# Two reorderings in a two-layer hybrid encoder: the third projection tile's weights are split ahead of the first row's scaling and convolution, and the closing norm takes the last row's squares as a second matmul operand

## The chip, the core and the metric

The kernel runs on one core of one Trainium2 chip. The number that counts is the device time of one execution in microseconds (us); the time of a kernel is the median of several executions. Of one execution there is also a profile: when each instruction ran on which engine, what it waited for, and the clock that the throttle granted to the matmul engine. The engines are PE (matmul; its weight loads are listed apart as PEld), DVE (vector), ACT (scalar, activation functions), POOL (GpSimd) and SP (which here only issues DMAs). Each engine works through its own instructions in a fixed order; an instruction that waits holds up all behind it on that engine.

## The reference

Sixteen learned tokens are put before the 1024 tokens of the input (1040 columns of 1024 channels), then two layers run, then a last norm:

```python
h = jnp.concatenate([meta, x], axis=1)
for l in range(DEPTH):
    h = h + hybrid_mixer(rmsnorm(h, norm1_w[l]), w_in[l], conv_qkv_w[l], ...)
    h = h + swiglu(rmsnorm(h, norm2_w[l]), w_gate_up[l], w_down[l])
h = rmsnorm(h, final_norm_w)
return h[:, N_META:]

def rmsnorm(x, w):
    return x * lax.rsqrt(jnp.mean(x * x, axis=-1, keepdims=True) + RMS_EPS) * w
```

In `hybrid_mixer` one projection gives q, k and v of four heads, among others; each of their channels goes through a convolution over three neighbouring tokens and a SiLU, and q and k are then scaled to length one per head:

```python
qkv = jax.nn.silu(depthwise_conv_centred(qkv, conv_qkv_w))
q, k, v = jnp.split(qkv, 3, axis=-1)
k = l2norm(k.reshape(Bsz, L, DN_HEADS, DN_HEAD_DIM))
```

All of it is float32.

## The kernel before

Channels lie on the 128 partitions and tokens in the free dimension, so a row of the kernel's text is a tile of 128 channels by 1040 tokens. A float32 matmul is made from three fast ones: each operand is split into a rounded part (`hi`) and the rest (`lo`), and `dense` (L144 to L171) sums hi*hi, hi*lo and lo*hi for eight blocks of 128 input channels. A projection tile is thus 24 matmuls for each of three column chunks (348, 346 and 346 wide).

The weights of a tile come in two halves of four blocks each. `wsplit` (L122) loads one half from memory (L127, on SP's queue), rounds it on ACT (L128, `whi<-raw`) and subtracts on DVE (L129, `wlo<-raw,whi`). There are three buffers each for `whi` and `wlo` and two for `raw`.

**The start of layer 0.** The scale of the first norm (`rstd`, one number for each token) needs the squares of all of x, and is there only after a chain of sums on PE (L259), a square root on ACT (L215), a reciprocal on DVE (L216) and two DMAs (L217, L219). Meanwhile the loop over `seq` (L644 on) projects tiles 4, 5, 6, 7 (the four k heads) and then 0 to 3 (q). For tiles 4 and 5 the sums are copied out unscaled (L307), and the whole row is scaled later (L653); from tile 6 on the scale is applied on the way out of PSUM (L302). After that the row goes through `conv`: ACT multiplies by the middle tap (L314), DVE adds the two neighbours (L315, L316). For k rows follow SiLU (L639) and the squares (L640) on ACT, and later, as a queued job, a short PE sum of these squares (`sums`, L613). With the fourth k head's sum, `normalise` takes the root (L415) and the reciprocal (L416), POOL's queue writes the lengths out and reads them back spread over the partitions (L418, L421), and DVE scales each k head (L422). `k_out` transposes k on PE (L430, for all four heads of 16 or 128 tokens each) and ACT copies the result out (L432); `chunk_p` multiplies k with itself (L458). After tile 6 the gates are computed (`gates`, L343 on, with its matmuls at L349).

**The end.** The last four blocks of the down projection and the final norm run by column chunk (`FIN`: 512, 256 and 256 columns wide) over eight rows m. For each row: 12 matmuls (L155 to L157), an add to the residual on DVE (L924), the squares on ACT (L186, L180 for the first row), their running sum in `ss` on DVE (L187), and a multiplication by the norm's weight on ACT (L1446). After eight rows `final_scale` sums `ss` over the partitions (PE, L196), takes root (L198) and reciprocal (L199), builds a diagonal (L201) and spreads it over the partitions by another matmul (L204, bank `bc`). DVE then multiplies the eight rows by it (L1450) and SP stores them in pairs (L1451).

**What sets the order.** The program is traced in this order, with priorities, and a scheduler (`schedule_with_timeline_sim=True`) then orders the instructions of each engine by its own forecast of when they can run. A small change in the text can so move instructions some hundred rows away. `after(ins, prev)` adds a dependency by hand: `ins` may not run before `prev`.

Of the kernel before, what the change touches and what calls it, by code (L numbers as in the profile page):

```python
# [7 lines left out]
F32 = mybir.dt.float32  # L8
# [3 lines left out]
ALU = mybir.AluOpType  # L12
# [30 lines left out]
def trunk(ctx: ExitStack, tc: tile.TileContext, xT, w_in, w_ba, w_out, w_gu, w_dn,  # L43
# [75 lines left out]
    evp = [None]  # L119
    jobs, jobs2, jobs3 = [], [], []  # L120

    def wsplit(src, hi, lo, raw=None):  # L122

        kk = src.shape[1]
        if raw is None:
            raw = wp.tile([128, WK, 128], F32, tag="raw", bufs=2, name=nm("raw"))
        dma(raw[:, 0:kk, :], src)  # L127
        act(out=hi, in_=raw[:, 0:kk, :], func=AF.Copy)  # L128
        tt(out=lo, in0=raw[:, 0:kk, :], in1=hi.bitcast(F32), op=ALU.subtract)  # L129

    def wload(src, nk):

# [55 lines left out]

    cols = {}

    def final_scale(ss, n0, n1):

        nt = (n1 - n0) // 128
        ps = bank("a")
        for j in range(nt):
            mm(ps[:, j:j + 1], ss[:, n0 + 128 * j:n0 + 128 * j + 128], ones[:, 0:1], start=True, stop=True)  # L196
        r = sb.tile([128, 4], F32, tag="st", bufs=2, name=nm("rt"))[:, 0:nt]
        act(out=r, in_=ps[:, 0:nt], func=AF.Sqrt, scale=1.0 / D, bias=cols["eps"])  # L198
        nc.vector.reciprocal(out=r, in_=r)  # L199
        dg = t2k("dg")[:, 0:nt, :]  # L200
        tt(out=dg, in0=ident.unsqueeze(1).to_broadcast([128, nt, 128]), in1=r.unsqueeze(2).to_broadcast([128, nt, 128]), op=ALU.mult)  # L201
        bc = bank("b")
        for j in range(nt):
            mm(bc[:, 128 * j:128 * j + 128], ones, dg[:, j, :], start=True, stop=True)  # L204
        return bc[:, 0:n1 - n0]

    def finish_bc(ss, n0, n1, dst, ps=None):

# [77 lines left out]
    for l in range(DEPTH):  # L286
# [23 lines left out]
        def trow():  # L310
            return row(Y[1], F32, 3)

        def conv(src, dst, wc):
            act(out=dst, in_=src, func=AF.Copy, scale=pcol(wc + 1))  # L314
            stt(out=dst[:, 1:L], in0=src[:, 0:L - 1], scalar=pcol(wc), in1=dst[:, 1:L], op0=ALU.mult, op1=ALU.add)  # L315
            stt(out=dst[:, 0:L - 1], in0=src[:, 1:L], scalar=pcol(wc + 2), in1=dst[:, 0:L - 1], op0=ALU.mult, op1=ALU.add)  # L316

# [320 lines left out]
        def lengths(which, q, row_, buf):  # L638
            act(out=row_, in_=row_, func=AF.Silu)  # L639
            act(out=buf, in_=row_, func=AF.Square)  # L640
            jobs.append(lambda: sums(which, q, buf))

        seq = (4, 5, 6, 7, 0, 1, 2, 3)
        for pos, i in enumerate(seq):  # L644
            hh = pos % 4
            if pos == 2:
                gate_weights()
                evp[0] = base - 60000
            t = trow()
            late = pos < (2, 1)[l]  # L650
            inproj(i, to_row_late(t) if late else to_row(t), pfirst if l == 0 and pos == 1 else None)
            if late:
                tt(out=t, in0=t, in1=rstd, op=ALU.mult)  # L653
# [258 lines left out]
        for i in range(4):  # L912
# [6 lines left out]
                tt(out=yl[:, n0:n1], in0=t[:, n0:n1], in1=yh[:, i, n0:n1].bitcast(F32), op=ALU.subtract)  # L919
            ys.append((yh[:, i, :], yl))  # L920

        def add_h(m, then=None):
            def f(ps, n0, n1):
                tt(out=hr[m][:, n0:n1], in0=ps, in1=hr[m][:, n0:n1], op=ALU.add)  # L924
                if then is not None:
                    then(n0, n1)
            return f
# [508 lines left out]
        if not last:  # L1436
            for m in range(KT):
                then = next_norm(m, x[m], par[:, (l + 1) * P_L + P_N1 + m:(l + 1) * P_L + P_N1 + m + 1], ss)
                dense(pre.pop(("dn", m)) if m < 2 else wload(w_dn[l, m, :, 2 * NP:FT, :], NF), rest, chunks, add_h(m, then), pwide)
                dma(hd[m], hr[m])  # L1440
        else:
            for (n0, n1) in FIN:
                for m in range(KT):
                    dense(wds[m], rest, [(n0, n1)], add_h(m), pwide)
                    add_sq(hr[m][:, n0:n1], ss[:, n0:n1], m == 0)
                    act(out=hr[m][:, n0:n1], in_=hr[m][:, n0:n1], func=AF.Copy, scale=par[:, 2 * P_L + m:2 * P_L + m + 1])  # L1446
                bc = final_scale(ss, n0, n1)
                for m in range(0, KT, 2):
                    for q in (m, m + 1):
                        tt(out=hr[q][:, n0:n1], in0=bc, in1=hr[q][:, n0:n1], op=ALU.mult)  # L1450
                    dma(out[m:m + 2, :, n0 - 16:n1 - 16].rearrange("m p t -> p m t"), hb[m // 4][:, m % 4:m % 4 + 2, n0:n1])  # L1451
        if not last:
            finish_bc(ss, 0, L, rsd[1])
        hsrc = hd
# [73 lines left out]
```

## Time and profile before

| | |
|---|---|
| median of 3 runs | 2509.69 us (2503.12 to 2511.69) |
| the profiled execution, its own time | 2505.71 us |
| its span in the trace | 2503.9 us |
| PE busy | 2468.2 us, 99% of the span |
| DVE, ACT, POOL busy | 1763.6, 1045.2, 145.7 us |
| granted clock, mean | 0.997 |

The span is what lies between the first and the last instruction of the trace; the execution's own time is 1.8 us longer. A row of the timeline gives the start, the duration, the engine, the line of the kernel, the operation, the output and the inputs by the program's names, and in brackets the idle time of the engine just before the row and what ended it. A float32 matmul that isn't split counts as two passes (`x8` stands for four of them). PE's rows overlap: the time from one start to the next is what one costs.

### The profile page before, as it was taken

The numbers are of one execution on the slowest core, as the hardware profiler recorded it, in microseconds if no ns is written. First come the engines' busy times: TensorE is split into PE (matmuls) and PEld (weight loads), VectorE is DVE, ScalarE is ACT, GpSimd is POOL, SyncE is SP. The second block draws the span as 40 slices with busy tenths as digits, with TensorE's granted clock in tenths as the row PEclk, the third lists the DMA queues.
The fourth block names the chain that finished last, engine by engine and source line by source line (L and its number), as shares of the span: only waits on it lengthen the run. The fifth ranks groups of instructions, "written<-read, shape, count | busy, mean of one in ns | idle before, by whom it ended". The sixth has DMA issues, their size and how long they took to land.

```text
span 2503.9 us, 44660 instructions
## 1 busy us (share of the span) xinstructions
PE 2468.2 (99%) x17468; PEld 2267.7 (91%) x17468; DVE 1763.6 (70%) x3224; ACT 1045.2 (42%) x1933; POOL 145.7 (6%) x222
## 2 busy tenths in 40 slices
PE   8999999999999999999999999999999999999998
PEld 6989999999999999999999988998978888888887
DVE  5688255769877777787666883457798777668775
ACT  5675222435333333444445752224453333334444
POOL 0040101001000000000000301010110000000000
PEclk9999999999999999999999999999999999999999
DMA  3453155623432222673323531456434322238541
GB/s 131 135 169 101 60 185 166 228 77 122 148 111 99 84 82 77 229 231 120 100 96 125 170 107 68 153 173 218 127 126 156 104 84 84 84 107 288 158 138 68
DMA packets 190887, 331.05 MB, mean 132 GB/s; under 512 B 22956, under 2 KB 77028, under 8 KB 190676
## 3 DMA queue, kind: packets, MB, share of 16 engines
q1 hardware_dynamic: 164676, 290.10, 35.3%
q10 hardware_dynamic: 20752, 25.28, 3.1%
q0 software_dynamic: 5248, 12.82, 1.5%
q8 instruction: 137, 2.24, 0.4%
q14 instruction: 74, 0.61, 0.1%
HBM read 250.31 MB, written 77.80 MB: 131 GB/s over the span
## 4 chain that ended last, share of the span: by engine, by line
PE 86%; DVE 3%; DMA 3%; ACT 2%; issue 1%; POOL 1%; SPq 0%; ACTq 0%; DVEq 0%; POOLq 0%
PE pacc L155 9%; PE pacc L157 9%; PE pacc L156 9%; PE pacc L1034 4%; PE pacc L1036 4%; PE pacc L1035 4%; PE pf L1036 3%; PE pf L1034 3%; PE pf L1035 3%; PE pb L1036 3%; PE pb L1034 3%; PE pb L1035 3%; PE pacc L1427 2%; PE pacc L1425 2%; PE pacc L1426 2%; PE pa L1034 1%
## 5 line engine op out<-in xcount | busy, mean ns | idle before, releaser
L155 PE MATMUL pacc<-a,whi 128*128 128x346 f32 (+1 forms) x808 | 263.5, 329 | 8.3 <-ACT whi L128 7.7
L157 PE MATMUL pacc<-a,wlo 128*128 128x346 f32 (+1 forms) x808 | 262.8, 327 | 0.6 <-DVE wlo L129 0.6
L155 PE MATMUL pacc<-b,whi 128*128 128x346 f32 (+2 forms) x672 | 234.1, 349 | 0.9 <-ACT b L918 0.9
L157 PE MATMUL pacc<-b,wlo 128*128 128x346 f32 (+2 forms) x672 | 231.7, 346 | 0.0
L128 ACT ACTIVATE whi<-raw 128x512 fp32r<-128x512 f32 x168 | 105.4, 629 | 291.9 <-PE pacc L156 243.6
L156 PE MATMUL pacc<-a,whi 128*128 128x346 f32 (+1 forms) x688 | 224.1, 326 | 0.0
L156 PE MATMUL pacc<-b,whi 128*128 128x346 f32 (+2 forms) x580 | 200.4, 346 | 0.4 <-DVE b L919 0.4
L155 PEld LDWEIGHTS pacc<-a,whi 128*128 128x128 f32 x808 | 152.4, 189 | 12.6 <-ACT whi L128 8.2
L129 DVE TENSOR_TENSOR wlo<-raw,whi 128x512 fp32r<-128x512 f32 x168 | 117.4, 699 | 64.3 <-ACT whi L128 63.6
L157 PEld LDWEIGHTS pacc<-a,wlo 128*128 128x128 f32 x808 | 152.5, 189 | 2.8 <-issue 1.3
L155 PEld LDWEIGHTS pacc<-b,whi 128*128 128x128 f32 x672 | 126.5, 188 | 10.7 <-issue 1.5
L157 PEld LDWEIGHTS pacc<-b,wlo 128*128 128x128 f32 x672 | 126.4, 188 | 9.3 <-issue 1.3
L156 PEld LDWEIGHTS pacc<-a,whi 128*128 128x128 f32 x688 | 130.0, 189 | 2.8 <-issue 2.4
L1016 ACT ACTIVATE whi<-rw 128x512 fp32r<-128x512 f32 x100 | 62.7, 631 | 154.3 <-DVE rw L1294 47.3
L156 PEld LDWEIGHTS pacc<-b,whi 128*128 128x128 f32 x580 | 109.2, 188 | 8.0 <-issue 0.8
L1016 ACT ACTIVATE b<-rw 128x512 fp32r<-128x512 f32 x64 | 40.2, 631 | 123.1 <-PE pacc L1035 41.8
L1016 ACT ACTIVATE a<-rw 128x512 fp32r<-128x512 f32 x64 | 40.0, 628 | 106.2 <-PE pacc L1035 70.3
L1017 DVE TENSOR_TENSOR wlo<-rw,whi 128x512 fp32r<-128x512 f32 x100 | 68.1, 684 | 4.9 <-ACT whi L1016 4.2
L302 DVE TENSOR_TENSOR a<-pacc,rstd 128x346 f32<-128x346 f32 (+2 forms) x59 | 32.7, 553 | 46.5 <-PE pacc L157 46.5
L302 DVE TENSOR_TENSOR b<-pacc,rstd 128x346 f32<-128x346 f32 (+1 forms) x63 | 32.2, 512 | 45.2 <-PE pacc L157 45.2
L821 DVE TENSOR_TENSOR rec<-rec 128x512 f32<-128x512 f32 x32 | 22.7, 710 | 46.6 <-DMA rec<-dtd 27.8
L1034 PE MATMUL pacc<-b,whi 128*128 128x260 f32 (+1 forms) x172 | 53.0, 308 | 1.9 <-ACT whi L1016 1.2
(981 smaller groups left out, 7923.1 us busy)
## 6 DMA issues: line engine op xcount, KB each, us to landing
raw<-in_w_in SPq DMA_DIRECT2D x112, 256.0 KB, 2.8
rw<-in_w_gu SPq DMA_DIRECT2D x96, 256.0 KB, 2.8
raw<-in_w_gu SPq DMA_DIRECT2D x96, 256.0 KB, 2.8
rec<-vkd SPq DMA_DIRECT2D x61, 256.0 KB, 3.0
rw<-in_w_dn SPq DMA_DIRECT2D x70, 192.0 KB, 3.6
raw<-in_w_out SPq DMA_DIRECT2D x48, 256.0 KB, 2.7
b<-ad SPq DMA_DIRECT2D x45, 260.0 KB, 4.2
a<-ad SPq DMA_DIRECT2D x45, 256.0 KB, 4.4
```

The lines of the kernel that those rows point to most:

```text
L128: act(out=hi, in_=raw[:, 0:kk, :], func=AF.Copy)
L129: tt(out=lo, in0=raw[:, 0:kk, :], in1=hi.bitcast(F32), op=ALU.subtract)
L155: mm(ps[:, :n], wh, xh[:, n0:n1], start=(k == 0), stop=False)
L156: mm(ps[:, :n], wh, xl[:, n0:n1], start=False, stop=False)
L157: mm(ps[:, :n], wl, xh[:, n0:n1], start=False, stop=(k == K - 1))
L302: tt(out=t[:, n0:n1], in0=ps, in1=rstd[:, n0:n1], op=ALU.mult)
L1016: act(out=hi, in_=src, func=AF.Copy)
L1017: tt(out=lo, in0=src, in1=hi.bitcast(F32), op=ALU.subtract)
L1034: mm(ps[:, :CW], w[0][:, k, :], th[:, cs], start=first and k == 0, stop=False, skip_group_check=True)
L1035: mm(ps[:, :CW], w[0][:, k, :], tl[:, cs], start=False, stop=False, skip_group_check=True)
L1036: mm(ps[:, :CW], w[1][:, k, :], th[:, cs], start=False, stop=stop and k == nk - 1, skip_group_check=True)
L1425: mm(ps[:, :CW], wh[:, k, :], th[:, cs], start=st, stop=False, skip_group_check=True)
```

## The change

First, `wsplit` keeps its two instructions in `lastw`. In layer 0 the work on the first row (tile 4) after its projection is held back as `held`; after the projection of the second row (tile 5) the weights of the third tile (6) are loaded and split, and only then `held` runs: the scaling of the first row is ordered behind the last `lo` of those weights, its convolution's ACT instruction behind the last `hi`.

Second, in the end stage the last row's squares are no longer added to `ss`. They stay in a tile `sq`, and `final_scale` takes `ss` and `sq` as two operands that PE sums in the same bank. The scaling of the second column chunk, which stood behind that chunk's `final_scale` in the text, is now written behind the last add of the third chunk.

```diff
+    lastw = [None, None]
     def wsplit(src, hi, lo, raw=None):
...
-        act(out=hi, in_=raw[:, 0:kk, :], func=AF.Copy)
-        tt(out=lo, in0=raw[:, 0:kk, :], in1=hi.bitcast(F32), op=ALU.subtract)
+        lastw[0] = act(out=hi, in_=raw[:, 0:kk, :], func=AF.Copy)
+        lastw[1] = tt(out=lo, in0=raw[:, 0:kk, :], in1=hi.bitcast(F32), op=ALU.subtract)
...
-    def final_scale(ss, n0, n1):
-        nt = (n1 - n0) // 128
+    def final_scale(parts):
+        nt = parts[0].shape[1] // 128
         ps = bank("a")
         for j in range(nt):
-            mm(ps[:, j:j + 1], ss[:, n0 + 128 * j:n0 + 128 * j + 128], ones[:, 0:1], start=True, stop=True)
+            for i, t in enumerate(parts):
+                mm(ps[:, j:j + 1], t[:, 128 * j:128 * j + 128], ones[:, 0:1], start=(i == 0), stop=(i == len(parts) - 1))
...
-        def conv(src, dst, wc):
-            act(out=dst, in_=src, func=AF.Copy, scale=pcol(wc + 1))
+        def conv(src, dst, wc, prev=None):
+            after(act(out=dst, in_=src, func=AF.Copy, scale=pcol(wc + 1)), prev)
...
-            if late:
-                tt(out=t, in0=t, in1=rstd, op=ALU.mult)
-            dst = (QT if i < 4 else KTt)[:, hh, :]
-            conv(t, dst, P_CV + 3 * i)
-            if i >= 4:
-                lengths("k", hh, dst, t)
+            def convolved(hi=None, lo=None, i=i, hh=hh, t=t, late=late):
+                if late:
+                    after(tt(out=t, in0=t, in1=rstd, op=ALU.mult), lo)
+                dst = (QT if i < 4 else KTt)[:, hh, :]
+                conv(t, dst, P_CV + 3 * i, hi)
+                if i >= 4:
+                    lengths("k", hh, dst, t)
+            if l == 0 and pos == 0:
+                held = convolved
+                continue
+            if l == 0 and pos == 1:
+                pre[seq[2]] = wload(w_in[l, seq[2]], KT)
+                held(*lastw)
+            convolved()
...
-                tt(out=hr[m][:, n0:n1], in0=ps, in1=hr[m][:, n0:n1], op=ALU.add)
+                added[0] = tt(out=hr[m][:, n0:n1], in0=ps, in1=hr[m][:, n0:n1], op=ALU.add)
...
-            for (n0, n1) in FIN:
+            bc = None
+            def scaled(n0, n1, prev):
+                for m in range(0, KT, 2):
+                    for q in (m, m + 1):
+                        after(tt(out=hr[q][:, n0:n1], in0=bc, in1=hr[q][:, n0:n1], op=ALU.mult), prev)
+                    dma(out[m:m + 2, :, n0 - 16:n1 - 16].rearrange("m p t -> p m t"), hb[m // 4][:, m % 4:m % 4 + 2, n0:n1])
+            for c, (n0, n1) in enumerate(FIN):
                 for m in range(KT):
                     dense(wds[m], rest, [(n0, n1)], add_h(m), pwide)
-                    add_sq(hr[m][:, n0:n1], ss[:, n0:n1], m == 0)
+                    prev = added[0]
+                    if m < KT - 1:
+                        add_sq(hr[m][:, n0:n1], ss[:, n0:n1], m == 0)
+                    else:
+                        sq = c4k("sq")[:, 0:n1 - n0]
+                        act(out=sq, in_=hr[m][:, n0:n1], func=AF.Square)
                     act(out=hr[m][:, n0:n1], in_=hr[m][:, n0:n1], func=AF.Copy, scale=...)
-                bc = final_scale(ss, n0, n1)
-                for m in range(0, KT, 2):
...
+                    if c == 2 and m == KT - 1:
+                        scaled(*FIN[1], prev)
+                bc = final_scale([ss[:, n0:n1], sq])
+                if c != 1:
+                    scaled(n0, n1, None)
```

Three places in the engines' order, before and after the scheduler has placed the changed text. Its line numbers are shifted by the added lines: L128 is now L130, L314 L317, L415 L418, L464 L467, L639 L642, L640 L643; at the end L924 is L939, L199 L202, L201 L204, L204 L207, L196 L199, L1450 L1462.

ACT at the start of layer 0. `whi_405` and `whi_411` (before), `whi_388` and `whi_394` (now) are the two halves of tile 6's weights, `whi_620` and `whi_626` those of tile 7's; `b_44` is the first row, `b_59` the second, `b_70` (now `b_69`) the third. Before:

```order
L128 ACTIVATE whi_405<-raw_407 128x512
L215 ACT_TABLE_LOAD
L215 ACTIVATE r_304<-pb_228,epsc 128x260
L314 ACTIVATE b_38_169<-b_44_175,par 128x1040
L128 ACTIVATE whi_411<-raw_413 128x512
L639 ACT_TABLE_LOAD
L639 ACTIVATE b_38_169<-b_38_169 128x1040
L640 ACTIVATE b_44_175<-b_38_169 128x1040
```

Now:

```order
L218 ACTIVATE r_304<-pb_228,epsc 128x260
L130 ACTIVATE whi_394<-raw_396 128x512
L130 ACTIVATE whi_620<-raw_622 128x512
L317 ACTIVATE b_38_169<-b_44_175,par 128x1040
L317 ACTIVATE b_38_169<-b_59_309,par 128x1040
L642 ACT_TABLE_LOAD
L642 ACTIVATE b_38_169<-b_38_169 128x1040
L643 ACTIVATE b_44_175<-b_38_169 128x1040
L130 ACTIVATE whi_626<-raw_628 128x512
```

The second half of tile 6's weights, which stood behind the first row's convolution, now stands ahead of it, and the second row's convolution follows at once. On PE the third chunk of tile 5 (24 matmuls, rows 214 to 237, behind tile 6 and part of the gates) now stands ahead of tile 6.

ACT where the k lengths are taken. `pf` holds the sums of squares of k, `b3f` their roots; `ptm` are tiles of the gates' decay, which get exponentials (L464). Before:

```order
L461 DMA ptm_886<-gd_157 16x4x16
L128 ACTIVATE whi_843<-raw_845 128x512
L461 DMA ptm_886<-gd_157 16x4x16
L415 ACT_TABLE_LOAD
L415 ACTIVATE b3f_763<-pf_342,epsc 128x260
L461 DMA ptm_886<-gd_157 128x512 x3
L464 ACT_TABLE_LOAD
L464 ACTIVATE ptm_886<-ptm_886,nGb_574 16x16 x4
```

Now:

```order
L464 DMA ptm_886<-gd_157 16x4x16 x2
L464 DMA ptm_886<-gd_157 128x512 x2
L130 ACTIVATE whi_843<-raw_845 128x512
L467 ACTIVATE ptm_886<-ptm_886,nGb_574 16x16 x6
L418 ACT_TABLE_LOAD
L418 ACTIVATE b3f_763<-pf_442,epsc 128x260
L467 ACT_TABLE_LOAD
L467 ACTIVATE ptm_886<-ptm_886,nGb_574 16x16 x2
```

Six exponentials now stand ahead of the square root.

DVE at the end of the kernel, from the last row's add on. `pb_24554` (now `pb_24558`) holds the second chunk's scale, `pb_24719` (now `pb_24724`) the third's. Before:

```order
L924 TENSOR_TENSOR b_2371_22792<-pacc_24693,b_2371_22792 128x256
L1450 TENSOR_TENSOR b_2370_22791<-pb_24554,b_2370_22791 128x256 x4
L1450 TENSOR_TENSOR b_2371_22792<-pb_24554,b_2371_22792 128x256 x4
L187 TENSOR_TENSOR rstd_24234<-rstd_24234,sq_24707 128x256
L199 RECIPROCAL rt_24714<-rt_24714 128x2
L201 TENSOR_TENSOR dg_24717<-ident,rt_24714 128x256
L1450 TENSOR_TENSOR b_2370_22791<-pb_24719,b_2370_22791 128x256 x4
```

Now:

```order
L939 TENSOR_TENSOR b_2371_22792<-pacc_24685,b_2371_22792 128x256
L1462 TENSOR_TENSOR b_2370_22791<-pb_24558,b_2370_22791 128x256 x4
L1462 TENSOR_TENSOR b_2371_22792<-pb_24558,b_2371_22792 128x256 x4
L202 RECIPROCAL rt_24719<-rt_24719 128x2
L204 TENSOR_TENSOR dg_24722<-ident,rt_24719 128x256
L1462 TENSOR_TENSOR b_2370_22791<-pb_24724,b_2370_22791 128x256 x4
```

The eight multiplications of the second chunk stand where they stood; the add of the last row's squares behind them is gone. On PE the second chunk's spreading matmuls (`pb_24558`), which stood behind the last matmul of the last row, now stand inside that row, with eight of its twelve matmuls behind them:

```order
L158 MATMUL pacc_24685<-b_2468_23830,a_2495_24126 128x256
L159 MATMUL pacc_24685<-b_2373_22794,a3f_24130 128x256
L157 MATMUL pacc_24685<-b_2373_22794,a_2495_24126 128x256
L207 MATMUL pb_24558<-dg_24556,ones 128x128 x2
L158 MATMUL pacc_24685<-b_2471_23877,a_2495_24126 128x256
```

More of the change, by code (lines that the diff above doesn't have):

```diff
@@ L204, in final_scale @@
             mm(bc[:, 128 * j:128 * j + 128], ones, dg[:, j, :], start=True, stop=True)
-        return bc[:, 0:n1 - n0]
+        return bc[:, 0:128 * nt]
     def finish_bc(ss, n0, n1, dst, ps=None):
@@ L920, in trunk @@
             ys.append((yh[:, i, :], yl))
+        added = [None]
         def add_h(m, then=None):
             def f(ps, n0, n1):
-                tt(out=hr[m][:, n0:n1], in0=ps, in1=hr[m][:, n0:n1], op=ALU.add)
+                added[0] = tt(out=hr[m][:, n0:n1], in0=ps, in1=hr[m][:, n0:n1], op=ALU.add)
                 if then is not None:
```

3 lines of the change are left out of this document (removed).

## The prediction, made before the changed kernel ran

> **What bounds the kernel now.** The page's first part comes first:
>
> ```profile
> PE 2468.2 (99%) x17468; PEld 2267.7 (91%) x17468; DVE 1763.6 (70%) x3224; ACT 1045.2 (42%) x1933; POOL 145.7 (6%) x222
> ```
>
> PE is busy for 99% of the span, so an edit on another engine can win only what PE waits. Neither part of the change takes a matmul away; the second adds some. The list of waits, for PE in the first 300 us, shows what is there to win:
>
> ```profile
> PE pacc L155 <- ACT whi L128: 7.7, 2, 5.4
> PE pa L430 <- ACT kt L432: 1.6, 2, 1.3
> PE pf L613 <- ACT sq L640: 1.1, 1, 1.1
> PE pa L430 <- DVE b L422: 1.0, 1, 1.0
> PE pacc L157 <- DVE wlo L129: 0.6, 2, 0.4
> ```
>
> Of the 7.7 us in the first row, 5.4 are the start, which the change leaves alone. The other 2.3 are in the timeline:
>
> ```profile
> 40.57 0.32 PE L156 MATMUL pacc<-a,whi 128*128 128x346 f32 x1
> 40.73 0.32 PE L157 MATMUL pacc<-a,wlo 128*128 128x346 f32 x1
> 43.33 0.43 PE L155 MATMUL pacc<-a,whi 128*128 128x348 f32 x1 [2.28 <-ACT whi L128]
> ...
> 44.75 0.43 PE L157 MATMUL pacc<-a,wlo 128*128 128x348 f32 x1 [0.20 <-DVE wlo L129]
> ```
>
> Matmuls start 0.16 us apart; then PE stands for 2.28 us until ACT has rounded the second half of tile 6's weights, and 0.20 more for the rest. ACT and DVE at that place:
>
> ```profile
> 40.32 1.24 DVE L653 TENSOR_TENSOR b<-b,rstd 128x1040 f32<-128x1040 f32 x1 [4.43 <-DMA rstd<-rsd]
> ...
> 41.59 1.16 ACT L314 ACTIVATE b<-b,par 128x1040 f32<-128x1040 f32 x1 [8.54 <-DVE b L653]
> 42.66 0.61 ACT L128 ACTIVATE whi<-raw 128x512 fp32r<-128x512 f32 x1
> ```
>
> ACT was idle for 8.54 us, with the weights queued behind a convolution that waited for the scaling, which waited for `rstd`. This is the wait that the first part attacks.
>
> **The first part: what goes.** The weights now stand ahead of the convolution. 2.28 + 0.20 = 2.48 us of PE's idle time go, if the split is in time. PE now does the third chunk of tile 5 (24 matmuls) ahead of tile 6, of which it had done 36 before the stall: it reaches tile 6 at 40.9 - 36 x 0.16 + 24 x 0.16 = 39.0, and needs the second half's weights 14 matmuls later, at 41.2.
>
> ```profile
> 32.58 0.48 ACT L215 ACTIVATE r<-pb,epsc 128x260 f32<-128x260 f32 x1
> ...
> 35.37 0.52 DVE L307 COPY b<-pacc 128x346 f32<-128x346 f32 x1 [0.51 <-PE pacc L157]
> ...
> 42.79 1.30 DVE L315 SCALAR_TENSOR_TENSOR b<-b,par,b 128x1039 f32<-128x1039 f32 x1 [1.23 <-ACT b L314]
> ...
> 45.98 1.28 ACT L639 ACT_TABLE_LOAD   x1 [2.71 <-DVE b L316]
> 47.28 1.07 ACT L639 ACTIVATE b<-b 128x1040 f32<-128x1040 f32 x1
> ```
>
> In the new order ten more matmuls stand ahead of the last sum of squares (row 114 of PE's list instead of 104), so the root ends 10 x 0.16 = 1.6 us later, at 34.7; the weights follow it on ACT (0.61, to 35.3), and their rest on DVE behind the copy of tile 5's second chunk, which moves by the same 1.6 us, to 37.5, so to 38.2. That is 3 us early. The stall goes.
>
> **What is late next.** `rstd` too comes 1.6 us later, at 41.9. From there DVE scales row one, subtracts the next tile's weights, scales row two, and does the first convolution (about 1.24 + 0.6 + 1.24 + 1.3 + 0.5 + 1.3, to some 47.9); ACT loads its table and does SiLU and squares (1.28 + 1.07 + 1.07), to 51.4. PE wants these squares (L613) 6 matmuls behind tile 6, at 39.0 + 78 x 0.16 = 51.5. This is just in time; I take 0, with 1 us as the upper bound. The evictions of tile 6 queue on DVE behind these two rows, but the three banks come free by 53, before PE needs them again at about 57.
>
> **Where the gain meets the next chain.** 50 us on, PE transposes the k heads, and each waits for DVE to scale it:
>
> ```profile
> 88.49 0.63 ACT L128 ACTIVATE whi<-raw 128x512 fp32r<-128x512 f32 x1 [1.33 <-PE pf L613]
> ...
> 90.44 0.48 ACT L415 ACTIVATE b3f<-pf,epsc 128x260 f32<-128x260 f32 x1
> 90.95 1.78 DVE L416 RECIPROCAL b3f<-b3f 128x260 f32<-128x260 f32 x1 [0.98 <-ACT b3f L415]
> ...
> 95.20 2.05 ACT L464 ACTIVATE ptm<-ptm,nGb 16x16 f32<-16x16 f32 x8
> ...
> 104.36 1.24 DVE L422 TENSOR_TENSOR b<-b,bc 128x1040 f32<-128x1040 f32 x1 [2.48 <-DMA bc<-rnd]
> 105.66 0.28 PE L430 MATMUL pa<-ident,b 128*16 128x128 f32 x1 [0.96 <-DVE b L422]
> 105.90 0.53 POOL L421 DMA_DIRECT2D bc<-rnd  x1 [7.09 <-DVE b L422]
> ...
> 111.52 1.24 DVE L422 TENSOR_TENSOR b<-b,bc 128x1040 f32<-128x1040 f32 x1 [1.28 <-DMA bc<-rnd]
> ...
> 113.05 0.27 PE L430 MATMUL pa<-ident,b 128*16 128x128 f32 x1
> ```
>
> Here the order costs. ACT gets to the weights at 88.49 - 2.48 = 86.0, but six exponentials (2.05 / 8 = 0.26 each) now come ahead of the root: 86.0 + 0.6 + 1.5 + 1.28 + 0.48 = 89.9. The reciprocal starts 1.0 us earlier than before, not 2.5, and so do the two DMAs behind it. First head: DVE at 103.35, PE at 104.65. PE, with nine more matmuls ahead of that transpose, gets there at 104.70 - 2.48 + 1.43 = 103.65, and waits 1.0 as it did before. Third head: its lengths are read back into a buffer that the first head frees, 5.6 us from POOL's issue (105.90) to DVE's start (111.52); 1.0 us earlier that is 110.5, ready at 111.8. PE arrives at 104.65 + 27 x 0.16 + 2 x 0.75 for two heads' matmuls = 110.5 and waits 1.3, where it had not waited. What is left of the gain is 113.05 - 111.8 = 1.2 us. Bounds: all 2.5 if the read-back is quicker; a loss, if the exponentials wait (a rival below).
>
> The later waits of the list (1.6 + 1.1 + 0.4 = 3.1 us) hang on ACT's order, which is dealt anew: k's copy comes ahead of a table load in one place, and behind two in the next. I take them as they were; bounds -3.1 and +1.
>
> **The second part.**
>
> ```profile
> 2466.00:2490.60 24.60, 24.60 (x212) 24.60 (x211) 17.99 (x42) 15.42 (x35) 0.00 (x0) 1.00 0.23 87
> ...
> 2494.10:2496.20 2.10, 1.01 (x4) 0.93 (x4) 0.62 (x3) 0.26 (x1) 0.00 (x0) 0.50 0.84 285
> ...
> 41.00:43.30 2.30, 0.05 (x1) 0.00 (x0) 1.07 (x2) 1.68 (x2) 0.00 (x0) 1.00 0.00 0
> ```
> ```profile
> 2470.51 0.94 PE L196 MATMUL pa<-ones,rstd 128*128 128x1 f32 x8
> 2471.31 0.36 PE L155 MATMUL pf<-b,a 128*128 128x256 f32 x1
> ...
> 2490.42 0.60 PE L204 MATMUL pb<-dg,ones 128*128 128x128 f32 x4
> 2490.62 0.42 DVE L924 TENSOR_TENSOR b<-pacc,b 128x256 f32<-128x256 f32 x1
> 2491.06 2.74 DVE L1450 TENSOR_TENSOR b<-pb,b 128x256 f32<-128x256 f32 x8
> 2491.08 0.42 ACT L186 ACTIVATE sq<-b 128x256 f32<-128x256 f32 x1 [0.45 <-DVE b L924]
> 2493.72 0.41 DVE L187 TENSOR_TENSOR rstd<-rstd,sq 128x256 f32<-128x256 f32 x1
> 2494.19 1.01 PE L196 MATMUL pa<-ones,rstd 128*128 128x1 f32 x4 [3.16 <-DVE rstd L187]
> ...
> 2495.53 0.17 DVE L199 RECIPROCAL rt<-rt 128x2 f32<-128x2 f32 x1 [1.40 <-ACT rt L198]
> ...
> 2496.21 1.22 PE L204 MATMUL pb<-dg,ones 128*128 128x128 f32 x4 [1.01 <-DVE dg L201]
> ```
>
> The first window (span, then busy time of PE, PEld, DVE, ACT, POOL, the clock) says that PE works without a gap up to the last row. Then the last sum stands on DVE behind eight multiplications (2.74) of the chunk before. Now PE takes the squares at 2491.08 + 0.42 = 2491.5, sums in about 0.9, and ACT has the root by some 2492.8, while DVE multiplies: the reciprocal starts when DVE is done, 2493.8 instead of 2495.53. That saves 1.7 us, counted from the last add.
>
> But the last add comes later. The extra operand doubles the sums: eight more passes for the first chunk, at (2471.31 - 2470.51) / 8 = 0.10 each 0.8, and four for the second 0.4, both in the middle of PE's gapless work; and the second chunk's spreading (2490.42, four passes, 0.4 at the same price) moves from behind the last row's matmuls into them. 0.8 + 0.4 + 0.4 = 1.6 us. The three adds taken off DVE are hidden already, since DVE waits for PE there. The end nets -1.7 + 1.6, about 0; bounds +0.3, for breaking into PE's flow once more, and -0.7, by the clock.
>
> The second window has it: the clock (third number from the end) was 0.50, with PE idle for 3.16 us ahead of it, and four passes took 1.01 and 1.22 us, where eight had taken 0.94. In the change PE waits about 1.0 us for the squares and about 2.1 us for the diagonal. In the third window, the stall of 2.28 us at the start, the granted clock was 1.00, so it may stay at full here: 1.22 - 0.60 = 0.6 us less. [...]
>
> **The sum.** -1.2 + 0 gives 2503.9 - 1.2 = 2502.7 us of span, 2505.71 - 1.2 = 2504.5 us for the profiled execution. That one lay 4.0 us below the median of its kernel, so the median goes from 2509.69 to **2508.5 us**.
>
> **The rivals.**
> - *The whole gain comes through*: the read-back is in time and two thirds of the later waits shrink, ACT being ahead: -2.5 - 2.0 = -4.5, 2505.2. For it: those waits are queueing on ACT. Against it: the third head's 5.6 us.
> - *The length chain decides, slower*: the six exponentials wait for their DMA rows and the root behind them ends 2.2 us later than before, not 1.0 earlier. Then the third head is ready at 111.52 + 2.2 + 1.24 = 115.0 against 113.05: +1.9, 2511.6. It decides once the root ends later than 89.9 + 1.2 = 91.1, since the third head moves with it and has 1.2 us to give. For it: root and table loads share one queue; against it: the gates run some 3 us earlier too.
> - *The clock stays full at the end*: -0.6 more, 2507.9.
> - *The stall only moves*: PE waits 1 us at the squares of row one (51.5) and meets the heads no earlier: 2509.7.
>
> Chances: forecast 0.38, whole gain 0.26, slower chain 0.18, clock 0.10, stall moved 0.08. About 0.3% (7.5 us) is what a measurement can tell from no change; no case reaches it, and only the scatter of the runs (2503.12 to 2511.69) can carry one there, downwards more easily: faster 0.14, within 0.77, slower 0.09. The range takes in -4.5 and +1.9 and 2 us or less of scatter at either end, 2503 to 2512.5.
>
> **What would show it.** Right: no PE wait for `whi` near 41; PE at the third k transpose 1 to 1.5 us earlier than 113.05, after a wait for DVE; reciprocal of the lengths at about 89.9; in the end PE's last row 1.6 us longer and the last reciprocal 2.8 us behind the last add. Wrong: a wait for squares near 51, a root later than 92, or PE's extra passes costing much more or less than 0.10 each.

## The result: 0.2% slower, and the profile after

| | before | after |
|---|---|---|
| median of 22 runs each, us | 2507.34 (2502.51 to 2511.69) | 2512.22 (2509.45 to 2515.54) |
| ratio of after to before | | 1.0021, 95% interval 1.0015 to 1.0027 |
| the profiled execution, us | 2505.71 | 2511.68 |
| its span, us | 2503.9 | 2509.9 |

The change costs about 5 us. The profile of after begins like this (busy time, share of the span and instructions of each engine):

```profile
PE 2473.5 (99%) x17484; PEld 2271.0 (90%) x17484; DVE 1763.6 (70%) x3221; ACT 1045.7 (42%) x1933; POOL 143.8 (6%) x222
```

PE's share is 99% as before, yet its busy time has grown by 5.3 us. Some of that are the 16 added rows (17484 for 17468). But PE's rows also overlap: at tile 6 they last 0.32 us and start 0.16 us apart, so one can start up to 0.16 us late without any idle time, and rows at half the clock simply last longer (128x346 matmuls 0.49 us each and 0.29 apart from 218.77 us on, at a granted clock of 0.50). So the share says little, and what has to be compared is when the same matmul starts in the two traces. The list of PE's waits in the first 300 us (us in total, times, longest):

```profile
PE pacc L157 <- ACT whi L130: 7.4, 2, 6.1
PE pa L433 <- ACT kt L435: 2.9, 2, 1.9
PE pacc L157 <- DVE b L305: 1.4, 1, 1.4
PE pb L461 <- DVE P L470: 0.6, 1, 0.6
PE pf L580 <- ACT P L573: 0.6, 1, 0.6
PE pa L433 <- DVE b L425: 0.4, 1, 0.4
```

6.1 us of the first row are the start. The stall at 41 us is gone, but there are new waits: for `b` (1.4), for `whi` in another place (7.4 - 6.1 = 1.3), for `P` twice, and those for `kt` have grown from 1.6 to 2.9 (the longest from 1.3 to 1.9). The new ones lie between 130 and 217 us.

The start itself, from the timeline of after (PE at tile 6 and at the squares of row one; ACT and DVE):

```profile
39.02 0.32 PE L157 MATMUL pacc<-a,whi 128*128 128x348 f32 x1
51.53 0.65 PE L616 MATMUL pf<-b,sel 128*32 128x260 f32 x8
39.06 0.63 ACT L130 ACTIVATE whi<-raw 128x512 fp32r<-128x512 f32 x1 [1.29 <-PE pf L158]
42.01 1.24 DVE L658 TENSOR_TENSOR b<-b,rstd 128x1040 f32<-128x1040 f32 x1 [2.27 <-DMA rstd<-rsd]
```

PE starts tile 6 at 39.02 and meets no wait up to the squares at 51.53. And the k heads (root, scaling of heads one and three, transpose of head three):

```profile
88.47 0.48 ACT L418 ACTIVATE b3f<-pf,epsc 128x260 f32<-128x260 f32 x1
102.09 1.24 DVE L425 TENSOR_TENSOR b<-b,bc 128x1040 f32<-128x1040 f32 x1 [2.94 <-DMA bc<-rnd]
108.41 1.24 DVE L425 TENSOR_TENSOR b<-b,bc 128x1040 f32<-128x1040 f32 x1 [0.91 <-DMA bc<-rnd]
109.71 0.28 PE L433 MATMUL pa<-ident,b 128*16 128x128 f32 x1 [0.38 <-DVE b L425]
```

The third head's transpose starts at 109.71, against 113.05 before: here the change is 3.3 us ahead. By the place that stands at 250 us before it is 4.2 us behind.

**Where it is lost.** Four matmuls can serve as marks: at 125.6, 152.1, 191.0 and 250.1 us in the trace of before, PE has done as many matmuls, of the same shapes and inputs, as at 122.4, 150.3, 192.1 and 254.3 us in the change. Between them lie stages A, B and C. The windows between the marks (stretch, length, then busy time and instructions of PE, PEld, DVE, ACT, POOL, the clock, DMA share, GB/s), before:

```profile
125.50:152.00 26.50, 23.78 (x177) 21.68 (x176) 20.93 (x31) 22.85 (x51) 21.59 (x58) 1.00 0.68 213
152.00:191.00 39.00, 38.60 (x257) 36.26 (x256) 33.54 (x72) 23.31 (x29) 6.32 (x12) 1.00 0.36 123
191.00:250.00 59.00, 59.00 (x745) 57.08 (x744) 49.56 (x117) 32.96 (x47) 2.27 (x2) 1.00 0.32 107
```

and after:

```profile
122.30:150.20 27.90, 24.24 (x177) 21.81 (x176) 20.85 (x31) 20.65 (x46) 20.48 (x60) 1.00 0.70 223
150.20:192.10 41.90, 39.18 (x257) 36.41 (x256) 36.10 (x78) 25.34 (x31) 6.32 (x12) 1.00 0.33 108
192.10:254.30 62.20, 61.64 (x745) 59.07 (x744) 47.90 (x110) 33.14 (x47) 2.35 (x2) 0.97 0.31 101
```

For the same matmuls PE needs 1.4, 2.9 and 3.2 us more: 7.5 in all. The fourth busy time is the one to read: in stage A ACT does 22.85 us of work before and 20.65 after, in stage B 23.31 and 25.34. Some 2 us of ACT's work have slid from A into B. In stage C the clock is 0.97, not 1.00: one stretch of 3.41 us at half rate (from 218.24 us, granted clock 0.50), which is told of at the end. The span grew by 6.0 us, not 4.2; the other 1.8 us came between 250 us and the closing stage. There the traces scatter from -2.6 to +3.0 us against before, whichever order they have (e3 below, of the old order, +3.0; e4, of the new, -1.0), so this part is not put down to the change.

**The closing stage.** The last matmul before, then after (last matmul and last add of the last row, sums, reciprocal, spreading):

```profile
2490.30 0.28 PE L157 MATMUL pacc<-b,a3f 128*128 128x256 f32 x1
```
```profile
2498.10 0.28 PE L159 MATMUL pacc<-b,a3f 128*128 128x256 f32 x1
2498.42 0.42 DVE L939 TENSOR_TENSOR b<-pacc,b 128x256 f32<-128x256 f32 x1 [0.53 <-PE pacc L159]
2499.35 0.38 PE L199 MATMUL pa<-ones,sq 128*128 128x1 f32 x2 [0.85 <-ACT sq L1473]
2501.54 0.15 DVE L202 RECIPROCAL rt<-rt 128x2 f32<-128x2 f32 x1
2502.21 1.22 PE L207 MATMUL pb<-dg,ones 128*128 128x128 f32 x4 [2.03 <-DVE dg L204]
```

The last matmul starts 2509.9 - 2498.10 = 11.8 us ahead of the end, against 2503.9 - 2490.30 = 13.6 before. But the last 192 projection matmuls (chunks two and three) take 26.5 us instead of 24.8. From the first of them to the end it is 38.3 us against 38.4 (38.0 to 38.4 in all the traces with the old closing stage): the closing stage nets nothing.

### The profile page after: what moved, and what is told of

It reads as the page before. It is cut to its first block, busy times and chain, and to the rows that moved or that the text cites. A ratio compares the mean times of both kernels' runs of the same rounds, so it can differ in the third digit from the quotient of the medians.

```text
span 2509.9 us, 44693 instructions
## 1 busy us (share of the span) xinstructions
PE 2473.5 (99%) x17484; PEld 2271.0 (90%) x17484; DVE 1763.6 (70%) x3221; ACT 1045.7 (42%) x1933; POOL 143.8 (6%) x222
## 4 chain that ended last, share of the span: by engine, by line
PE 86%; DMA 4%; DVE 4%; ACT 3%; issue 2%; POOL 0%; ACTq 0%; SPq 0%; DVEq 0%; POOLq 0%
PE pacc L157 9%; PE pacc L158 9%; PE pacc L159 9%; PE pacc L1049 4%; PE pacc L1051 4%; PE pacc L1050 4%; PE pf L1051 3%; PE pf L1049 3%; PE pf L1050 3%; PE pb L1051 3%; PE pb L1049 3%; PE pb L1050 3%; PE pacc L1442 2%; PE pacc L1440 2%; PE pacc L1441 2%
## 5 line engine op out<-in xcount | busy, mean ns | idle before, releaser
L130 ACT ACTIVATE whi<-raw 128x512 fp32r<-128x512 f32 x168 | 105.2, 629 | 297.5 <-PE pacc L158 246.2
L834 DVE TENSOR_TENSOR rec<-rec 128x512 f32<-128x512 f32 x32 | 22.9, 715 | 46.7 <-DMA rec<-dtd 27.0
```

The source lines that it names most:

```text
L130: lastw[0] = act(out=hi, in_=raw[:, 0:kk, :], func=AF.Copy)
```

## The experiments

The theory after the two traces: part one wins about 3 us at the start; the scheduler, which places everything by its own forecast, then hands out another order for the rest of layer 0, and that order is the slower one; part two nets nothing. All kernels below were timed in five rounds against the kernel before, whose median in the four groups of runs was 2507.83, 2509.1, 2509.08 and 2507.61 us; hence the ratios.

**e1 and e2: the parts apart.** e1 is the change with the closing stage put back; e2 puts back the start. The cores of the two edits, against the change:

```diff
-                bc = final_scale([ss[:, n0:n1], sq])
+                bc = final_scale(ss, n0, n1)
```
```diff
-            if l == 0 and pos == 1:
-                pre[seq[2]] = wload(w_in[l, seq[2]], KT)
-                held(*lastw)
-            convolved()
+            if late:
+                tt(out=t, in0=t, in1=rstd, op=ALU.mult)
...
```

> Part one alone; the closing stage is as before. Theory (the loss lies in the order that part one leaves behind it in layer 0, the closing stage nets nothing): as slow as the change, 2507.3 + 5 = about 2512 us, ratio 1.0015 to 1.0027, and PE's first 250 us with the same waits as the change (kt 2.9, b 1.4, whi 1.3 beside the start). Rival (the extra summing passes of the closing stage cost what was lost): no slower than before, 2504 to 2507 us.

> Part two alone; the start of layer 0 is as before. Theory: the same as before within 1 us, 2506.3 to 2508.3 us, the last matmul of the last row about 1.6 us later and the end 1.8 us closer behind it. Rival (the summing passes cost the loss): about 2512 us.

e1: 2513.15 us, ratio 1.0018 (1.0009 to 1.0027). e2: 2508.15 us, 1.0000 (0.9991 to 1.0009). In e2 the last 192 projection matmuls take 26.5 us and the last one starts 11.8 us ahead of the end, as in the change. e1's waits are those of the change (`b` 1.3, `whi` 7.4 - 6.1 = 1.3, `kt` 3.7 where 2.9 was expected), with 1.2 us each for `b` from DVE (0.4 in the change) and from ACT (none in the change). The loss is part one's alone. The rival is out.

**e3 and e4: start and order apart.** A list of instruction names for each of PE, ACT, DVE and POOL is laid over the program as ordering edges; it starts at 62 us and takes nothing away:

```diff
+def pin(tc, table):
+    info = mybir.DependencyInfo(mybir.DependencyClass.NoSync, mybir.DependencyReason.DATA)
+    here = {i.name: i for i in tc.nc.cur_bb.bb.instructions}
+    for text in table.values():
...
+        for a, b in zip(row, row[1:]):
+            tc.add_manual_dep(here[f"I-{b}"], f"I-{a}", info, reason="order")
```

e3 has part one's start and from 62 us on the old order, row for row; e4 the old start and the change's order.

> Part one at the start, but from 62 us on each of PE, ACT, DVE and POOL works in the order of the kernel before (ordering edges only, no instruction more or less; the closing stage as before). Theory (part one wins 2.5 to 3.9 us at the start, and the order behind it loses more): the gain stays, 2503.4 to 2504.8 us, no kt wait of 1.9 us near 141 and no half-rate stretch near 218. Rival (what is won is given back in any order, since DMAs and ACT set the pace of the k heads and of what follows): 2507 us, with the gain gone by 180 us.

> The mirror: the start as before up to 62 us, from there on each of PE, ACT, DVE and POOL in the order that the change has (the closing stage as before). Theory (the order as such is the slower one): slower than the change by what part one wins at the start, 2513 to 2516 us. Rival (the new waits come only of PE being some 3 us early, so that a PE that comes late meets none): 2507 to 2509 us.

e3: 2504.53 us, ratio 0.9990 (0.9981 to 0.9999): faster than before. e4: 2513.81 us, 1.0031 (1.0019 to 1.0042). The four kernels of this square add up: the new start is worth 0.0010 with the old order and 1.0031 - 1.0018 = 0.0013 with the new one (2.5 and 3.3 us); the new order costs 1.0018 - 0.9990 = 0.0028 with the new start and 0.0031 with the old (7.0 and 7.8 us), each with some 3 us of uncertainty. So the waits do not come of PE being early: with the old start PE comes late and meets them too.

**Where in the order?** f1, f2 and g1 have the change's order up to a seam (150, 192, 122 us) and the old one from there; g2 the old order up to 125 us and the change's from there.

> Part one with the change's order up to 150 us and from there, on PE, ACT, DVE and POOL, the order of the kernel before (ordering edges only; closing stage as before). Theory, by stages of the traces so far (new order against old: about +1.5 us from 125 to 152, +3 from 152 to 191, +1.7 from 191 to 250): 4.7 us less than part one alone (2513.15), about 2508.5 us; PE's waits for b and whi near 158 and 161 gone, those for kt near 133 and 141 still there. Rival (the loss is made ahead of 150, or a later order cannot take it back): 2511 to 2514 us.

> The same with the seam at 192 us. Theory: 1.7 us less than part one alone, about 2511.5 us, the waits for b and whi near 158 and 161 there again, the wait for P near 216 gone. Rival (most of the loss lies behind 192): 2505 to 2508 us.

> Part one with the change's order up to 122 us and from there the order of the kernel before (edges only; closing stage as before). Theory, mended after the seam at 150 us had not brought the time back: what is lost is ACT's time. Between PE's places of 125 and 152 us ACT does 22.9 us of work in the kernel before and 20.7 in the change, and PE pays these arrears later, whichever row stands first by then. So with the seam at 122, ahead of the arrears, nearly all comes back: 2504 to 2506 us, ratio 0.998 to 0.9995, ACT's work between those places 22 us or more. Rival (the arrears are there by 122): ratio 1.001 or more.

> The mirror: part one's start, the old order from 62 to 125 us, and the change's order from there. Theory (the order behind 122 to 125 us makes the arrears): as slow as part one alone, ratio 1.0012 to 1.003, ACT's work between PE's places of 125 and 152 us below 21.5 us. Rival (it is the order from 62 to 122 us): ratio below 0.9995.

f1: 2512.63 us, ratio 1.0015 (1.0006 to 1.0023), a miss. f2: 2510.6 us, 1.0008 (0.9999 to 1.0016). g1: 2506.2 us, 0.9988 (0.9979 to 0.9997). g2: 2510.78 us, 1.0009 (1.0000 to 1.0018), less than expected and still slower than e3 and g1. In f1 the rival came true: with the old order back from 150 us the time did not come back. f2 came about as expected; it lies below f1, but within the two intervals. With the seam at 122 the time did come back. So what stage B loses is set up between 122 and 150 us and only collected later. The stages of these and the next two traces, worked out as above from the starts of the four marks (in brackets the half-rate stretches that fell into the stage; each has a granted clock of 0.50 for 3.41 us and costs, by an estimate from these two numbers, up to 1.7 us):

| kernel | order in A, B, C | A | B | C | ACT's work in A, B |
|---|---|---|---|---|---|
| before | old, old, old | 26.5 | 39.0 | 59.0 | 22.9, 23.2 |
| e2 | old, old, old | 26.2 | 38.9 | 59.0 | 22.5, 23.1 |
| e3 | old, old, old | 25.7 | 39.2 | 59.0 | 22.0, 23.5 |
| f4 | old, old, old | 26.3 | 38.9 | 59.0 | 22.3, 23.1 |
| g1 | old, old, old | 28.6 (1) | 38.8 | 59.0 | 23.6, 23.1 |
| the change | new, new, new | 27.9 | 41.8 | 62.2 (1) | 20.7, 25.2 |
| e1 | new, new, new | 28.3 | 41.7 | 60.7 | 21.4, 25.1 |
| e4 | new, new, new | 27.5 | 42.2 (1) | 60.7 | 20.1, 25.5 |
| f3 | new, new, new | 30.3 (1) | 42.2 (1) | 60.7 | 20.3, 25.7 |
| g2 | new, new, new | 28.8 (1) | 40.9 | 60.7 | 21.4, 24.3 |
| f2 | new, new, old | 28.3 | 42.5 | 59.0 | 20.2, 25.9 |
| f1 | new, old, old | 31.0 (1) | 42.2 (1) | 59.0 | 22.7, 24.6 |

With 1.7 us taken off for each bracket, the means are 26.3 and 28.0 us for stage A (f1 left out), 39.0 and 41.3 for B, 59.0 and 60.7 for C. The new order costs 1.7 + 2.3 + 1.7 = 5.7 us. Stage C is a matter of its own: whoever has the old order there takes 59.0, whoever has the new one 60.7 (the change 62.2 with its half-rate stretch), without exception; the one wait in it is that for `P` (0.6). Stages A and B belong together, as f1 shows: the old order in B still took 40.5 without its half-rate stretch.

**f3: three rows moved.** In stage B the queue in front of the waits is plain to see in the change (ACT; then DVE; then PE):

```profile
148.87 8.55 ACT L523 ACTIVATE b<-P 32x1024 f32<-32x1024 f32 x8 [2.57 <-DVE b L319]
157.44 0.60 ACT L435 ACTIVATE kt<-pa 128x512 f32<-128x512 f32 x1
158.06 1.28 ACT L642 ACT_TABLE_LOAD   x1
160.33 1.13 ACT L130 ACTIVATE whi<-raw 128x512 fp32r<-128x512 f32 x2
157.06 0.51 DVE L305 TENSOR_TENSOR b<-pacc,rstd 128x346 f32<-128x346 f32 x1
157.62 0.43 PE L157 MATMUL pacc<-a,whi 128*128 128x346 f32 x1 [1.43 <-DVE b L305]
160.99 0.43 PE L157 MATMUL pacc<-a,whi 128*128 128x348 f32 x1 [1.29 <-ACT whi L130]
```

Eight long copies (of blocks of `P`, the products of k with itself times their decay) take ACT 8.55 us; the weights for which PE waits at 160.99 stand behind them, a copy, a table load and a SiLU. In before, the table load, the SiLU and the squares (L640) stand ahead of the same copies:

```profile
148.38 1.28 ACT L639 ACT_TABLE_LOAD   x1 [0.50 <-DMA raw<-in_w_in]
149.68 1.07 ACT L639 ACTIVATE b<-b 128x1040 f32<-128x1040 f32 x1
150.78 1.07 ACT L640 ACTIVATE sq<-b 128x1040 f32<-128x1040 f32 x1
151.76 8.53 ACT L520 ACTIVATE b<-P 32x1024 f32<-32x1024 f32 x8
```

So why not move the weights? f3 is e1 with its order pinned and three rows moved up in the lists: on ACT a copy `kt` by six places and the weights `whi` by one, past the SiLU with its table load; on DVE one eviction (`b` from `pacc`) by three places.

> Part one alone in the change's order throughout, but for three rows: on ACT the copy kt stands ahead of the table load and the exponentials that it followed near 138, and the weights whi ahead of the table load near 158; on DVE one eviction (b from pacc) stands four short steps earlier near 157. Theory (those three waits are queueing behind rows that need not be ahead): waits of 1.85, 1.29 and 0.77 us go, 3.9 us less than part one alone, about 2509.3 us. Rival (DMAs and ACT's sum of work set the pace there, so the waits come back a few us later): 2512 to 2514 us, and as much waiting by 250 us.

f3: 2514.19 us, ratio 1.0021 (1.0012 to 1.0030). Nothing won; the rival is right. The wait for `whi` went, those for `kt` (2.6) and `b` (1.0) mostly stayed, and in the list of PE's waits of f3 there is a new one:

```profile
PE pf L615 <- ACT sq L642: 3.2, 1, 3.2
```

The squares had to come behind what was moved ahead of them. Whichever of these rows stands first, PE waits for ACT. That gave the theory its second form: ACT is in arrears when stage B begins.

**h1 and h2: take the arrears away.** If so, less work on ACT must help in the new order, with every other row where it stands, and must not help in the old one. In both, four of the eight long copies go to POOL, in layer 0 alone:

```diff
                 for b in range(4):
-                    act(out=dg[B[b]], in_=Pv[d][B[b], :, B[b]], func=AF.Copy)
+                    if d == 1 and l == 0:
+                        nc.gpsimd.tensor_copy(dg[B[b]], Pv[d][B[b], :, B[b]])
+                    else:
+                        act(out=dg[B[b]], in_=Pv[d][B[b], :, B[b]], func=AF.Copy)
```

h1 is e1 so relieved, h2 is e3, both with their order pinned.

> Part one alone in the change's order throughout, but in layer 0 four of the eight long copies (1.07 us each) that stand ahead of k's copy, a table load and the weights on ACT near 153 are done by POOL, which is idle there. Nothing else changes its place. Theory (PE's waits from 152 to 191 are ACT's arrears): ACT is 4.3 us lighter ahead of those rows, the wait for whi near 161 (1.3) goes, and that stage takes 39.5 to 40.5 us instead of 41.7; the stages from 125 to 152 (28.0) and from 191 to 250 (60.7) stay; about 1.5 us less than part one alone, ratio 1.0007 to 1.0018. Rival (the order of PE's or DVE's own rows makes the waits): 41.7 us in that stage as before, ratio 1.0015 to 1.0025.

> The control: the start of part one, the old order from 62 us on, and the same four copies on POOL. Theory: there are no arrears to take away (that stage took 38.8 to 39.2 us in five runs of the old order, 38.6 of them busy), so 38.6 to 39.2 us again and the time of that kernel without the relief, ratio 0.998 to 0.9997. Rival (ACT bounds the stage in either order): below 38 us.

h1: 2509.2 us, ratio 1.0009 (1.0001 to 1.0018). h2: 2503.83 us, 0.9989 (0.9980 to 0.9998). Stage B of e1, then the stages of h1, from the windows between their marks:

```profile
153.70:195.40 41.70, 39.10 (x257) 36.31 (x256) 36.34 (x79) 25.18 (x31) 6.31 (x12) 1.00 0.32 110
```
```profile
125.00:153.70 28.70, 25.48 (x177) 23.17 (x176) 19.89 (x29) 21.86 (x47) 23.39 (x62) 0.94 0.73 232
153.70:192.40 38.70, 38.70 (x258) 36.43 (x257) 36.42 (x80) 19.17 (x25) 7.56 (x14) 1.00 0.31 102
192.40:254.60 62.20, 61.63 (x745) 59.05 (x744) 47.60 (x108) 33.17 (x47) 2.28 (x2) 0.97 0.31 100
```

Stage B takes 38.7 us where e1 took 41.7, with PE busy from end to end, in the same order on PE and DVE. That is more than expected: the wait for DVE's eviction went as well. Stages A and C stay near the new order's 28.0 and 60.7 (27.0 and 60.5 without the half-rate stretch that each has). Over the whole kernel h1 lies 0.0009 below e1, which is less than the two intervals can tell; the stage tells it. In h2, stage B takes 38.9 us, as in the five other traces of the old order. So in stage B it is ACT's arrears that PE pays, and they exist in the new order alone.

**f4: what the experiments point to.** Part one's start, the old order from 62 us, and the second operand only where it is on the path to the end:

```diff
-                    if m < KT - 1:
+                    if m < KT - 1 or c < 2:
                         add_sq(hr[m][:, n0:n1], ss[:, n0:n1], m == 0)
...
-                bc = final_scale([ss[:, n0:n1], sq])
+                bc = final_scale([ss[:, n0:n1], sq] if c == 2 else [ss[:, n0:n1]])
```

> The start of part one, the old order from 62 us on, and in the closing stage the second operand for the last column chunk alone (chunks one and two are summed as before; the second chunk's scaling behind the last add as in the change). Theory (the tail wins 1.8 us behind the last matmul and gives 1.4 to 1.7 us back in the extra passes of chunks one and two and the moved spreading): 1.4 to 1.8 us less than the start alone (2504.5), about 2502.9 us, ratio to before 0.998. Rival (the tail's gain needs the moved spreading): 2504.5 us.

f4: 2504.66 us, ratio 0.9981 (0.9971 to 0.9990): faster than both kernels. Its end, in the timeline:

```profile
2492.71 0.28 PE L159 MATMUL pacc<-b,a3f 128*128 128x256 f32 x1
2493.02 0.42 DVE L939 TENSOR_TENSOR b<-pacc,b 128x256 f32<-128x256 f32 x1
2496.21 0.16 DVE L202 RECIPROCAL rt<-rt 128x2 f32<-128x2 f32 x1
2496.88 0.71 PE L207 MATMUL pb<-dg,ones 128*128 128x128 f32 x4 [2.10 <-DVE dg L204]
```

The last 192 projection matmuls take 24.8 us again, the reciprocal stands 3.2 us behind the start of the last add (3.1 in the change), and the end comes 2504.1 - 2492.71 = 11.4 us behind the last matmul. The closing stage takes 36.2 us instead of 38.0 to 38.4. Of that, 0.5 us is put down to chance: the four spreading passes took 0.71 us here, and 1.22 in the change, where the granted clock was 0.50 from 2501.76 us on. The median, 2504.66, is the time that the rival named, but the kernel before took 2509.1 us in this group and 2507.83 in e3's, so only the ratio can be compared. It is 0.0009 lower than e3's, which is less than the two intervals can tell; that the closing stage is shorter, the trace shows.

## Why the prediction was wrong, point by point

**The stall and what is late next: right, in kind and size.** PE was to reach tile 6 at 39.0 and did at 39.02; `rstd` was to come at 41.9 and came at 42.01; the squares of row one were to be just in time at 51.5 and PE took them at 51.53 without a wait.

**The k heads: right in mechanism, too dark in size.** The root did stand behind six exponentials. The reciprocal started at 89.64 for a forecast of 89.9. Then both DMA legs were quicker than the rows of before: the first head was scaled 12.45 us behind the reciprocal, not 13.41, and the third head's read-back took 4.8 us from POOL's issue (103.63) to DVE's start, not 5.6. The third transpose came at 109.71 where 111.8 was forecast: 3.3 us of gain were left, not 1.2. That is more than the bound of 2.5, since the first head's wait of 0.96 us, which the prediction kept, went too (its transpose started at 103.39 without a wait).

**The step that failed: "The later waits of the list (1.6 + 1.1 + 0.4 = 3.1 us) hang on ACT's order, which is dealt anew ... I take them as they were; bounds -3.1 and +1."** Stages A and B, in which these waits lie, and C behind them took 7.5 us longer in this profile, 5.7 in the mean of the traces once the half-rate stretches are taken off. In place of the old waits stood longer ones (`kt` 2.9, `b` 1.4, `whi` 1.3): ACT did some 2 us less work in stage A, and PE paid for it in stage B, as h1 shows. The prediction saw that ACT's order was dealt anew and still priced it at nothing, and its upper bound held one microsecond for 120 us of changed order on four engines. A warning was at hand: in the kernel before, ACT was busy for 22.85 of the 26.5 us of stage A (86%), against 23.31 of 39.0 us in stage B (60%). An engine so full has little room to lose time in, and the new order makes it idle there. One such row is in the fence of f3: ACT is idle for 2.57 us with the copies at the head of its queue. In the order of before, a table load, a SiLU and the squares stood ahead of the copies, and the idle time ahead of those was 0.50 us.

**The second part: right.** The reciprocal was to stand 2.8 us behind the end of the last add and stood 2.7 (3.1 behind its start); PE's gapless stretch was to grow by 1.6 and grew by 1.7; the end behind the last matmul was to shrink by 1.7 and shrank by 1.8; the sum was 0, as forecast. f4 shows that the 1.6 us were avoidable.

**The rivals.** The slower length chain named 2511.6 us, close to the result, but by a mechanism that did not happen: the root was 2 us earlier than before, not 2.2 later. The clock did not stay at full at the end: the four spreading passes took 1.22 us again, at a granted clock of 0.50 from 2501.76 us on, behind a wait of 2.03. The stall did not move to the squares. The whole gain came through as far as 122 us and was lost behind it: the later waits grew where that rival had them shrink.

**The range.** The measured 2512.22 us lies just inside 2503 to 2512.5, and that is luck. The upper end came from the slower length chain and the scatter, and the sum started from a median of three runs, 2509.69, where 22 runs give 2507.34. The forecast was 1.2 us down, and the time went 4.9 us up.

**What stays open.** Which row between 122 and 150 us starts the arrears was not singled out: f3's three were not it. One place differs in all the traces alike. In the eight with the new order in stage A, ACT is idle for 1.65 to 3.23 us right ahead of the eight copies, and the table load, the SiLU and the squares come behind them (in f1 behind the first two). In the six with the old order those three come ahead of the copies, after 0.39 to 0.77 us of idle time. No run moved these rows alone, so that they are the cause is not shown. What makes stage C 1.7 us longer is known only as to its place, and that one wait of 0.6 us is part of it. The stages add up to 5.7 us of the 7.0 to 7.8 that e1 to e4 give for the order; the rest is within the uncertainty of those ratios. The half-rate stretches that were taken off may be part of it: in stages A to C there are nine in the eight traces with the new order and one in the six with the old; between 62 us and stage A it is one with the new order there and four with the old.

## What to carry to other kernels

When an edit makes a scheduler deal a new order, the edit's own arithmetic covers only the rows up to where the orders part; what lies behind needs a price of its own, and the stage where an off-path engine is fullest is where to look for it. Moving single rows of the full engine only moved the wait here; taking work off that engine brought 3 us back, and pinning the old order behind the edit brought back all. An extra operand in a sum pays only in the one chunk whose sum is on the path to the end.

## What the runs showed of the hardware

**The granted clock fell to 0.50 for 3.41 us at a time, and a stall could so cost more than its own length.** Up to 2488 us the trace of before has one stretch at a granted clock of 0.50, from 660.61 us, and that of the change two, from 218.24 and 665.39; each is 3.41 us long. At the end a longer one runs from 2493.57 us in before and from 2501.76 in the change, past the last instruction. The traces first record a full clock at 12.08 and 10.03 us, and every stretch begins a whole number of steps of 3.4133 us later: 648.53 us (190 steps) and 2481.49 (727) in before, 208.21 (61), 655.36 (192) and 2491.73 (730) in the change. The same stall at tile 6, in windows of one step, in before and in e2, whose start is the same program:

```profile
39.39:42.80 3.41, 1.66 (x11) 1.37 (x9) 1.25 (x2) 1.21 (x2) 0.00 (x0) 1.00 0.04 11
42.80:46.21 3.41, 2.69 (x15) 2.40 (x16) 3.10 (x3) 0.70 (x2) 0.00 (x0) 1.00 0.15 35
```
```profile
41.23:44.64 3.41, 1.02 (x7) 0.73 (x5) 1.68 (x2) 1.63 (x2) 0.00 (x0) 1.00 0.02 5
44.64:48.06 3.42, 3.32 (x11) 3.32 (x12) 2.67 (x3) 0.72 (x2) 0.00 (x0) 0.50 0.25 71
```

In before, the 2.28 us fall into two windows and the clock stays at 1.00. In e2 nearly all of the stall falls into one, PE is busy for 1.02 us of it, and the next window runs at 0.50, with matmuls 0.29 us apart instead of 0.16: by an estimate up to 1.7 us more (half of 3.41). PE's busy time in a window at full clock, and the clock granted in the next; of before and the change these are all the windows with less than 1.9 us behind the first full clock:

| kernel | window from, us | PE busy, us | clock in the next |
|---|---|---|---|
| f1 | 142.49 | 0.60 | 0.50 |
| before | 2490.16 | 0.87 | 0.50 |
| the change | 2498.35 | 0.98 | 0.50 |
| e2 | 41.23 | 1.02 | 0.50 |
| e1 | 141.20 | 1.54 | 1.00 |
| the change | 661.98 | 1.58 | 0.50 |
| before | 657.20 | 1.62 | 0.50 |
| the change | 139.74 | 1.63 | 1.00 |
| before | 39.39 | 1.66 | 1.00 |
| the change | 129.50 | 1.80 | 1.00 |

The stretch of the change in stage C followed a window in which PE was busy for 2.85 us, with 64 matmuls of 32 by 32 among them:

```profile
214.83:218.24 3.41, 2.85 (x70) 2.58 (x69) 3.21 (x9) 2.87 (x5) 0.00 (x0) 1.00 0.06 17
218.24:221.66 3.42, 3.42 (x15) 3.42 (x14) 3.18 (x8) 1.84 (x4) 0.00 (x0) 0.50 0.62 202
```

e1 has the same order there and a granted clock of 1.00 in the whole stage (60.7 us, against 62.2 in the change), so in one execution this stretch is chance. How a stall lies to the windows differs from run to run, as in before and e2; that this accounts for some of the scatter is an estimate of the author's. In e2 the half-rate stretch is right behind the stall, so there, by the same estimate, removing it would have been worth more than its 2.5 us.

**POOL copies about as fast as ACT here.** The four copies of 32 by 1024 took POOL 4.28 us in h2 (1.07 each) and 4.45 in h1; the other four took ACT 4.25 and 4.27.
